# Zero-padded lower query tiles in the stick-breaking scores of a streaming encoder step

## The chip, the cores and the metric

The kernel runs on one NeuronCore of a Trainium2 chip. The metric is the device time of one execution in microseconds (us), the median of several runs. The engines are named as the profile names them: PE is TensorE's matrix multiply and PEld its load of the stationary operand, DVE is VectorE, ACT is ScalarE, POOL is GpSimd and SP is SyncE, which here only issues DMAs.

## The reference, cut to what matters

One layer of a hybrid encoder is computed for a prompt (1024 frames) and for 8 running streams (16 new frames each): an input projection, a spatial-gating branch, a stick-breaking attention with 8 heads of dimension 64, an output projection, a memory cross-attention and a SwiGLU. All is float32. What the change touches is the scores of the prompt's stick-breaking attention:

```python
z = jnp.einsum('bqhd,bkhd->bhqk', q, k) * (SB_HEAD_DIM ** -0.5)
mask = k_pos[None, :] < q_pos[:, None]
log_keep = jnp.where(mask, jax.nn.log_sigmoid(-z), 0.0)
between = lax.cumsum(log_keep, axis=3, reverse=True) - log_keep
a = jnp.where(mask, jnp.exp(jax.nn.log_sigmoid(z) + between), 0.0)
o = jnp.einsum('bhqk,bkhd->bqhd', a, v)
```

## The kernel before, in words

Float32 precision is reached with products of a rounded type (fp32r): each operand is split into an upper part, the rounded value, and a lower part, the rest, and two or three of the four products are summed in PSUM.

The queries of the prompt are written to a DRAM scratch `q_d[c, n, row, token]`: `c` counts pairs of heads, `n` is 0 for the upper and 1 for the lower part, and of the 128 rows the first 64 belong to the even head of the pair and the last 64 to the odd one. `k_d` has the keys in the same form. `head_in(h)` (lines 189 to 206) loads one head's operands with DMAs on SP's queue:

- `khl` (128 x 1024): the upper keys in the 64 rows that are the head's own (0 to 63 for an even head, 64 to 127 for an odd one), the lower keys in the other 64 rows.
- `qhh` (128 x 1024): the upper queries twice, in both halves.
- `ql` (128 x 1024): the lower queries of both heads of a pair, loaded once per pair by one DMA of 512 KB when the even head comes. Like `khl` and `qhh` it has two buffers.
- `vhl`: the values of both heads.

In `chunk` (line 423) the scores of 128 queries against a run of `w` keys (128 to 512) are two products in one PSUM bank (lines 430 and 431). The first, over 128 rows, has `qhh` as its stationary operand and `khl` as the moving one; it gives upper queries times upper and lower keys. The second contracts over the head's own 64 rows alone (`es`) and gives lower queries times upper keys. A head has 12 such chunks: 2 of 128 keys, 2 of 256, 2 of 384 and 6 of 512. With 8 heads that makes 96 pairs of products.

Behind them a chunk goes through a chain of engines (`sticks`, lines 391 to 408): DVE adds the causal mask, ACT takes two sigmoids, DVE scans the products (line 403), POOL multiplies (line 405), PE transposes the result (line 389, tile `tr`), ACT and DVE split it into `ath` and `atl` (line 126 and 127), and PE multiplies it by the values (`av`).

The order of the work is set by the loop at lines 726 to 742. Each turn starts one new chunk (or one stream of the 8) and takes every active one a step further; a chunk's transposes follow its scores by two turns (`LAG`). The rest of a turn is filled with products of other work (`memory` and then `merge_a`, tiles `acc`) until the turn has spent 4700 counted columns of PE time. The count takes the columns of a product, at least 256, and not its rows. `head_in(h + 1)` is called when head `h` begins (line 705, from head 1 on), that is when all score products of head `h - 1` have been issued, so that its loads wait for those to release a buffer and have the time of head `h` to land. The loads of heads 0 and 1 are issued earlier, beside the gating branch (lines 316 and 317). The framework that fills the engines' queues may place an instruction ahead of its place in the program where its inputs come earlier.

Of the kernel before, what the change touches and what calls it, by code (L numbers as in the profile page):

```python
# [9 lines left out]
F32 = mybir.dt.float32  # L10
F32R = mybir.dt.float32r
# [5 lines left out]
P = 128  # L17
# [4 lines left out]
NP = 1024  # L22
# [15 lines left out]
def stream_step(ctx: ExitStack, tc: tile.TileContext, I, O, cst):  # L38
    nc = tc.nc

    def pool(stack, name, bufs=1, **kw):
        return stack.enter_context(tc.tile_pool(name=name, bufs=bufs, reuse_waits="tile", **kw))
# [10 lines left out]
    def nm(s):  # L53
        uid[0] += 1
        return f"{s}_{uid[0]}"
# [5 lines left out]
    def ps(tag, shape):  # L61
        n = next(cur[tag])
        return psum[0].tile(shape, F32, tag=f"bank{n}", name=nm(tag))
# [17 lines left out]
    q_d = dram.tile([4, 2, P, TOK], F32, name="q_d")  # L81
# [39 lines left out]
    def split(hi, lo, src, gain=None):  # L121
        if gain is not None:
            nc.scalar.activation(hi, src, AF.Copy, scale=gain)
            nc.vector.scalar_tensor_tensor(out=lo, in0=src, scalar=gain, in1=hi.bitcast(F32), op0=ALU.mult, op1=ALU.subtract)
            return
        nc.scalar.copy(hi, src)  # L126
        nc.vector.tensor_tensor(out=lo, in0=src, in1=hi.bitcast(F32), op=ALU.subtract)  # L127
# [56 lines left out]

    stB = ctx.enter_context(ExitStack())
    bhp = pool(stB, "b_h", bufs=2, side="right")
    vhls, qls, got = [], [], {}

    def head_in(h):
        e, c2 = h % 2, h // 2  # L190
        if e == 0:
            ql = bhp.tile([P, NP], F32R, tag="ql", name=nm("ql"))
            nc.sync.dma_start(ql.bitcast(F32), q_d[c2, 1, :, 0:NP])
            qls.append(ql)
        es = slice(e * 64, e * 64 + 64)
        qhh = bhp.tile([P, NP], F32R, tag="qhh", name=nm("qhh"))
        khl = bhp.tile([P, NP], F32R, tag="khl", name=nm("khl"))
        for n in range(2):
            half = slice(n * 64, n * 64 + 64)
            nc.sync.dma_start(khl[half].bitcast(F32), k_d[c2, n ^ e, es, 0:NP])  # L200
            nc.sync.dma_start(qhh[half].bitcast(F32), q_d[c2, 0, es, 0:NP])
        if e == 0:
            vhl = bhp.tile([P, 8, 2, P], F32R, tag="vhl", name=nm("vhl"))
            nc.sync.dma_start(vhl.bitcast(F32), v_d[:, h:h + 2, :].rearrange("(n p) e d -> p n e d", p=P))
            vhls.append(vhl)
        got[h] = qhh, qls[-1], khl, vhls[-1]

    with ExitStack() as st:
        banks(acc=(1, 2), tr=(3, 4), z=(5, 6))
# [100 lines left out]
        for m in range(2):  # L310
# [3 lines left out]
            nc.vector.tensor_tensor(out=wsT[:, m], in0=tr, in1=trilT.unsqueeze(1).broadcast_to([P, 4, P]), op=ALU.mult)  # L314

        head_in(0)
        head_in(1)

        def sgu_v(i):
# [49 lines left out]
    with ExitStack() as st:  # L369
# [12 lines left out]
        def mm(out, lhsT, rhs, start, stop):  # L382
            n = math.prod(out.shape[1:])
            spent[0] += max(256, n) if rhs.dtype != F32 else 2 * max(256, 2 * n)
            nc.tensor.matmul(out, lhsT=lhsT, rhs=rhs, start=start, stop=stop)  # L385

        def tp_(out, in_, idn):
            spent[0] += 261
            nc.tensor.transpose(out, in_, idn)  # L389

        def sticks(w, zmm, right=None):
            beta = sp.tile([P, 512], F32, tag="beta", name=nm("beta"))
            pr = sp.tile([P, 513], F32, tag="pr", name=nm("pr"))
            z = ps("z", [P, 512])[:, :w]
            for _ in zmm(z):
                yield
            yield beta, pr
            nc.scalar.activation(z_keep(z, beta[:, :w]), z, AF.Sigmoid, scale=-0.125)
            if right is None:
                nc.gpsimd.memset(pr[:, w:w + 1], 1.0)  # L400
            else:
                nc.gpsimd.tensor_copy(pr[:, w:w + 1], right[:, 0:1])
            nc.vector.tensor_tensor_scan(out=pr[:, :w][:, ::-1], data0=z[:, ::-1], data1=zero1.broadcast_to([P, w]),  # L403
                                         initial=1.0 if right is None else right[:, 0:1], op0=ALU.mult, op1=ALU.add)
            nc.gpsimd.tensor_tensor(out=beta[:, :w], in0=beta[:, :w], in1=pr[:, 1:w + 1], op=ALU.mult)  # L405
            yield
            for _ in range(LAG - 1):
                yield
# [5 lines left out]
        def pair(h, c, got):  # L414

            sh = {}
            spans = [(512, 2 * c), (0, 2 * c)] if c >= 2 else [(0, 2 * c)]
            for part, (s, _) in enumerate(spans):
                for qb in (2 * c, 2 * c + 1):
                    e = (qb + 1) * P if part == 0 else 512  # L420
                    yield chunk(h, c, qb, s, e, part, len(spans) - 1, sh, got)

        def chunk(h, c, qb, s, e, part, last, sh, got):
            qhh, ql, khl, vhl = got[h]
            ev = h % 2
            es, col = slice(ev * 64, ev * 64 + 64), slice((qb % 2) * P, (qb % 2) * P + P)
            w, qs = e - s, slice(qb * P, (qb + 1) * P)

            def zmm(z):
                mm(z, lhsT=qhh[:, qs], rhs=khl[:, s:e], start=True, stop=False)  # L430
                mm(z, lhsT=ql[es, qs], rhs=khl[es, s:e], start=False, stop=True)
                if part == 0:
                    nc.vector.tensor_tensor(out=z[:, w - P:w], in0=z[:, w - P:w], in1=causal, op=ALU.add)
                return ()

            for step in sticks(w, zmm, sh.get(qb)):
                if step:
                    beta, sh[qb] = step
                yield
            if qb % 2 == 0:  # L440
                sh["ath"] = tp.tile([P, 4, 256], F32R, tag="ath", name=nm("ath"))
                sh["atl"] = tp.tile([P, 4, 256], F32R, tag="atl", name=nm("atl"))
            ath, atl = sh["ath"], sh["atl"]
            n = w // P
            tr = ps("tr", [P, 4, P])
            for j in range(n):
                tp_(tr[:, j, :], beta[:, j * P:(j + 1) * P], ident)
            split(ath[:, :n, col], atl[:, :n, col], tr[:, :n, :])
            yield
            if qb % 2 == 0:  # L450
                return
            if part == 0:
                sh["av"] = ps("av", [P, 256])
            av = sh["av"]
            for j in range(n):
                lo = P if part == 0 and j == n - 1 else 0
                for m, at in enumerate((ath, atl)):
                    mm(av[:, lo:], lhsT=vhl[:, s // P + j, ev, :], rhs=at[:, j, lo:],
                                     start=part == 0 and j == 0 and m == 0, stop=part == last and j == n - 1 and m == 1)
            yield  # L460
            if part == last:
                oe = sp.tile([P, 256], F32, tag="oe", bufs=1, name=nm("oe"))
                nc.scalar.copy(oe[0:64], av[64:128])
                nc.vector.tensor_tensor(out=oe[0:64], in0=av[0:64], in1=oe[0:64], op=ALU.add)
                nc.sync.dma_start(oT_d[h * 64:h * 64 + 64, c * 256:(c + 1) * 256], oe[0:64])
# [234 lines left out]
        def tasks():  # L700
            sgot[0] = stream_in(0)
            n, b = 0, 0
            for h in range(8):
                if 0 < h < 7:
                    head_in(h + 1)
                for c in range(4):
                    for g in pair(h, c, got):
                        yield g
                        n += 1
                        if n == S0 + SP * b and b <= B:  # L710
                            yield stream(b, sgot) if b < B else stream_tails(sgot[B])
                            b += 1
                        elif b and n == S0 + SP * (b - 1) + LAG + 6 and b <= B:
                            sgot[b] = stream_in(b)
# [637 lines left out]
```

## Time and profile before

| | |
|---|---|
| median of 3 runs | 1779.42 us (1777.08 to 1784.06) |
| the profiled execution | 1778.3 us, of which the span of the instructions is 1776.5 us |
| PE busy | 1718.3 us, 97% of the span |
| PEld busy | 1501.5 us, 85% |
| DVE busy | 987.3 us, 56% |
| ACT busy | 678.2 us, 38% |
| POOL busy | 435.4 us, 25% |
| the stick-breaking stage | 283 to 578 us of the span |

A busy PE isn't a PE at its peak: matmuls overlap their neighbours, so the duration of one is longer than the time to the next one's start. The time that an instruction takes from its engine is read from the starts of its followers. A weight load (PEld) can run beside the matmul ahead of it, and where one doesn't, its start coincides with that of its own matmul.

### The profile page before, as it was taken

What the parts mean: (1) busy time and instruction counts of PE and PEld (TensorE: products, weight loads), DVE (VectorE), ACT (ScalarE), POOL (GpSimd) and SP (SyncE); (2) the same over time, 40 slices, a digit from 0 to 9 for tenths busy, and PEclk for the clock granted to TensorE, in tenths of its full rate; (3) what the DMA queues carried; (4) which work ended last, traced back from release to release, by engine and by line L of the source; (5) the groups of instructions that cost most, each with busy time, mean ns of one, the idle gap of its engine ahead of it and who ended that gap; (6) DMA issues with size and microseconds to landing.
All of it is one profiled execution on the core that took longest, in us unless ns stands there. A gap on an engine that the chain in (4) does not pass through costs nothing.

```text
span 1776.5 us, 26280 instructions
## 1 busy us (share of the span) xinstructions
PE 1718.3 (97%) x10039; PEld 1501.5 (85%) x10039; DVE 987.3 (56%) x1481; ACT 678.2 (38%) x1326; POOL 435.4 (25%) x572
## 2 busy tenths in 40 slices
PE   8999999999999999998799799999999999999997
PEld 6889887776777799998687699999999999888886
DVE  5312446889778746455635855555555556544444
ACT  5322224767556436445522433333333333011123
POOL 2101233444333320000011444443444442000002
PEclk9999998999999999999899899999999999999999
DMA  8457236567543634344633122222222226322202
GB/s 287 148 187 257 68 125 193 154 195 231 184 117 113 209 107 131 116 127 141 210 119 119 48 75 75 75 75 75 75 75 75 75 80 239 141 101 101 101 13 95
DMA packets 175070, 227.94 MB, mean 128 GB/s; under 512 B 12065, under 2 KB 122273, under 8 KB 174945
## 3 DMA queue, kind: packets, MB, share of 16 engines
q1 hardware_dynamic: 143248, 161.89, 30.0%
q10 hardware_dynamic: 23504, 35.79, 5.5%
q0 software_dynamic: 8192, 28.58, 4.3%
q8 instruction: 80, 1.31, 0.3%
q14 instruction: 46, 0.37, 0.1%
HBM read 161.86 MB, written 64.36 MB: 127 GB/s over the span
## 4 chain that ended last, share of the span: by engine, by line
PE 65%; DVE 4%; DMA 2%; issue 2%; ACT 2%; POOL 1%; SPq 0%; POOLq 0%; ACTq 0%; DVEq 0%
PE pp L1158 27%; PE tr L131 5%; PE tr L130 5%; PE tr L132 5%; PE acc L385 3%; PE acc L130 2%; PE acc L131 2%; PE acc L132 2%; PE pp L130 2%; PE z L385 2%; PE pp L131 2%; PE pp L132 2%; PE tr L389 2%; PE av L385 1%; PE ov L943 1%
## 5 line engine op out<-in xcount | busy, mean ns | idle before, releaser
L1158 PE MATMUL pp<-b,wg 128*128 128x288 f32 x1584 | 223.3, 297 | 2.2 <-ACT b L126 1.9
L1158 PEld LDWEIGHTS pp<-b,wg 128*128 128x128 f32 x1584 | 215.2, 189 | 2.9 <-ACT b L126 2.3
L131 PE MATMUL tr<-wd,hid 128*128 128x512 f32 x396 | 154.6, 391 | 0.0
L132 PE MATMUL tr<-wd,hid 128*128 128x512 f32 x396 | 154.1, 389 | 0.0
L130 PE MATMUL tr<-wd,hid 128*128 128x512 f32 x396 | 151.5, 389 | 0.9 <-DVE t L1148 0.9
L127 DVE TENSOR_TENSOR wg<-s,wg 128x512 fp32r<-128x512 f32 x88 | 87.7, 996 | 103.4 <-ACT wg L126 102.5
L1293 DVE TENSOR_TENSOR xr<-tr,xr 128x512 f32<-128x512 f32 x108 | 73.3, 689 | 121.0 <-PE tr L132 117.6
L405 POOL TENSOR_TENSOR beta<-beta,pr 128x512 f32<-128x512 f32 (+4 forms) x104 | 95.6, 921 | 163.8 <-DVE pr L403 147.6
L130 PE MATMUL acc<-wh,hah 128*128 128x512 f32 x288 | 114.5, 398 | 2.6 <-ACT hah L126 2.6
L132 PE MATMUL acc<-wh,hal 128*128 128x512 f32 x288 | 113.7, 395 | 0.6 <-DVE hal L127 0.6
L131 PE MATMUL acc<-wl,hah 128*128 128x512 f32 x288 | 113.1, 393 | 0.0
L126 ACT CAST hid<-hr 128x576 fp32r<-128x576 f32 x44 | 27.3, 668 | 188.7 <-PE tr L132 177.8
L126 ACT CAST wg<-raw 128x512 fp32r<-128x512 f32 x66 | 41.0, 622 | 132.3 <-PE pp L1158 54.4
L130 PEld LDWEIGHTS tr<-wd,hid 128*128 128x128 f32 x396 | 74.4, 188 | 17.0 <-DVE t L1148 1.1
L131 PEld LDWEIGHTS tr<-wd,hid 128*128 128x128 f32 x396 | 74.3, 188 | 16.7 <-DVE wd L127 1.5
L132 PEld LDWEIGHTS tr<-wd,hid 128*128 128x128 f32 x396 | 74.4, 188 | 15.3
L126 ACT CAST wg<-s 128x512 fp32r<-128x512 f32 x88 | 54.2, 620 | 76.3 <-PE pp L1158 43.3
L1015 POOL DMA_DIRECT2D x_d<-xt x9 | 5.6, 627 | 312.8 <-DVE xt L1014 312.8
L1305 POOL TENSOR_SCALAR sm<-sm 128x1 f32<-128x1 f32 x9 | 7.1, 794 | 253.1 <-ACT junk L1298 253.1
L1078 POOL TENSOR_TENSOR s<-raw 128x512 f32<-128x512 f32 x22 | 28.9, 1315 | 156.0 <-DMA raw<-in_w_ffn_up_dram 75.4
L385 PE MATMUL acc<-mw,aT 128*128 128x512 f32 x216 | 66.8, 421 | 0.1
L127 DVE TENSOR_TENSOR wl<-raw,wh 128x1024 fp32r<-128x1024 f32 x36 | 43.7, 1221 | 41.0 <-ACT wh L126 40.4
(281 smaller groups left out, 4555.4 us busy)
## 6 DMA issues: line engine op xcount, KB each, us to landing
hid_d<-g ACTq DMA_DIRECT2D x44, 288.0 KB, 2.1
hr<-hid_d SPq DMA_DIRECT2D x44, 288.0 KB, 4.7
raw<-in_w_ffn_gate_dram SPq DMA_DIRECT2D x22, 512.0 KB, 3.9
raw<-in_w_ffn_up_dram SPq DMA_DIRECT2D x22, 512.0 KB, 4.0
raw<-in_w_ffn_down_dram SPq DMA_DIRECT2D x22, 512.0 KB, 4.5
raw<-in_w_in_dram SPq DMA_DIRECT2D x20, 512.0 KB, 5.1
x_d<-xt POOLq DMA_DIRECT2D x18, 512.0 KB, 3.1
raw<-in_cache_mem_k_dram SPq DMA_DIRECT2D x16, 512.0 KB, 4.4
```

Source lines behind the costliest of these rows:

```text
L126: nc.scalar.copy(hi, src)
L127: nc.vector.tensor_tensor(out=lo, in0=src, in1=hi.bitcast(F32), op=ALU.subtract)
L130: nc.tensor.matmul(out, lhsT=lh, rhs=rh, start=first, stop=False)
L131: nc.tensor.matmul(out, lhsT=lh, rhs=rl, start=False, stop=False)
L132: nc.tensor.matmul(out, lhsT=ll, rhs=rh, start=False, stop=last)
L385: nc.tensor.matmul(out, lhsT=lhsT, rhs=rhs, start=start, stop=stop)
L389: nc.tensor.transpose(out, in_, idn)
L405: nc.gpsimd.tensor_tensor(out=beta[:, :w], in0=beta[:, :w], in1=pr[:, 1:w + 1], op=ALU.mult)
L943: nc.tensor.matmul(ov[:, g], lhsT=pm[:, n, g, b4 * P:(b4 + 1) * P], rhs=vv[m][:, n], start=b4 == 0 and n == 0 and m == 0, stop=b4 == 3 and ...
L1078: nc.gpsimd.tensor_tensor(out=s[n], in0=x, in1=y, op=op)
L1158: nc.tensor.matmul(acc[:, h], lhsT=hl[:, a, c], rhs=b[:, c, h * TN:(h + 1) * TN], start=c == 0 and k == 0, stop=c == 3 and k == 2)
L1293: nc.vector.tensor_tensor(out=xr[i][:, hs], in0=pd, in1=xr[i][:, hs], op=ALU.add)
```

## The change

The lower queries stand in two fixed tiles, `qz0` for even heads and `qz1` for odd ones, each 128 x 1024 with one buffer. The half that isn't the head's own is set to zero once by POOL, when heads 0 and 1 are loaded. Each head loads its own 64 rows by a DMA of 256 KB, ahead of its `khl` and `qhh`. The second product of the scores then contracts over all 128 rows.

```diff
+    qzs = [bhp.tile([P, NP], F32R, name=f"qz{e}", bufs=1) for e in range(2)]
-    vhls, qls, got = [], [], {}
+    vhls, got = [], {}
 
     def head_in(h):
         e, c2 = h % 2, h // 2
-        if e == 0:
-            ql = bhp.tile([P, NP], F32R, tag="ql", name=nm("ql"))
-            nc.sync.dma_start(ql.bitcast(F32), q_d[c2, 1, :, 0:NP])
-            qls.append(ql)
         es = slice(e * 64, e * 64 + 64)
+        if h < 2:
+            nc.gpsimd.memset(qzs[e][64 - e * 64:128 - e * 64].bitcast(F32), 0.0)
+        nc.sync.dma_start(qzs[e][es].bitcast(F32), q_d[c2, 1, es, 0:NP])
...
-        got[h] = qhh, qls[-1], khl, vhls[-1]
+        got[h] = qhh, qzs[e], khl, vhls[-1]
...
-            es, col = slice(ev * 64, ev * 64 + 64), slice((qb % 2) * P, (qb % 2) * P + P)
+            col = slice((qb % 2) * P, (qb % 2) * P + P)
...
                 mm(z, lhsT=qhh[:, qs], rhs=khl[:, s:e], start=True, stop=False)
-                mm(z, lhsT=ql[es, qs], rhs=khl[es, s:e], start=False, stop=True)
+                mm(z, lhsT=ql[:, qs], rhs=khl[:, s:e], start=False, stop=True)
```

## Rows read from the trace of the kernel before

**Rows 1.** Windows, one per head: length, busy PE, PEld, DVE, ACT, POOL; clock, DMA.

```profile
283.00:325.43 42.43, 38.27 (x170) 26.99 (x168) 35.70 (x59) 28.10 (x61) 18.71 (x32) 0.88 0.68 216
325.43:363.32 37.89, 37.60 (x221) 28.24 (x219) 32.70 (x55) 26.37 (x62) 16.03 (x33) 1.00 0.54 152
363.32:399.44 36.12, 35.44 (x198) 25.90 (x196) 30.30 (x52) 24.42 (x56) 13.96 (x28) 1.00 0.71 215
399.44:429.48 30.04, 28.40 (x161) 19.24 (x159) 27.11 (x50) 23.39 (x55) 14.42 (x27) 1.00 0.69 217
429.48:465.78 36.30, 36.16 (x207) 26.59 (x205) 30.62 (x54) 21.39 (x52) 14.93 (x32) 1.00 0.76 231
465.78:501.35 35.57, 35.41 (x201) 26.07 (x199) 26.94 (x49) 19.55 (x48) 12.83 (x29) 1.00 0.46 141
501.35:539.04 37.69, 37.31 (x209) 26.80 (x208) 28.91 (x52) 19.42 (x49) 13.88 (x33) 1.00 0.42 120
539.04:578.30 39.26, 37.68 (x201) 28.39 (x201) 34.43 (x62) 24.34 (x52) 13.13 (x20) 1.00 0.34 110
```

**Rows 2.** Tile z: the lower products, duration in ns, first and last start, shapes.

```profile
L385 PE MATMUL z<-khl,ql x96: 322/491/792, 283.4 to 569.0; 64*128 64x512 f32 x48, 64*128 64x128 f32 x16, 64*128 64x256 f32 x16, 64*128 64x384 f32 x16
```

**Rows 3.** Timeline of PE, a pair of 512 keys: start us, duration us, instruction.

```profile
567.19 1.64 PE L385 MATMUL acc<-mw,aT 128*128 128x512 f32 x6
568.66 0.40 PE L385 MATMUL z<-khl,qhh 128*128 128x512 f32 x1
568.99 0.50 PE L385 MATMUL z<-khl,ql 64*128 64x512 f32 x1
569.42 0.55 PE L389 MATMUL tr<-csb,beta 128*128 128x128 f32 x3
```

**Rows 4.** Timeline of PEld, the weight loads of the same pair; in brackets idle before.

```profile
568.44 0.19 PEld L385 LDWEIGHTS z<-khl,qhh 128*128 128x128 f32 x1
568.99 0.18 PEld L385 LDWEIGHTS z<-khl,ql 64*128 64x128 f32 x1 [0.36 <-issue]
```

**Rows 5.** Timeline of PE, pairs of 128 and 256 keys, neighbours of those widths.

```profile
547.52 0.28 PE L385 MATMUL av<-ath,vhl 128*128 128x256 f32 x1
547.64 0.28 PE L385 MATMUL av<-atl,vhl 128*128 128x256 f32 x1
...
549.95 0.22 PE L385 MATMUL z<-khl,qhh 128*128 128x128 f32 x1
...
550.35 0.44 PE L389 MATMUL tr<-csb,beta 128*128 128x128 f32 x2
...
552.44 0.28 PE L385 MATMUL z<-khl,qhh 128*128 128x256 f32 x1
...
552.96 0.55 PE L389 MATMUL tr<-csb,beta 128*128 128x128 f32 x3
...
553.58 0.22 PE L385 MATMUL av<-ath,vhl 128*128 128x128 f32 x1
553.64 0.28 PE L385 MATMUL av<-atl,vhl 128*128 128x128 f32 x1
553.76 0.44 PE L385 MATMUL acc<-mw,aT 128*128 128x512 f32 x1
```

**Rows 6.** Waits of PEld, 283 to 578: waiter <- releaser, us, times, longest.

```profile
PEld z L385 <- issue: 28.1, 97, 0.7
```

**Rows 7.** Chain of waits behind the stage: start us, us, what.

```profile
578.30 5.57 DMA xt<-xa_d
```

**Rows 8.** Timeline of SP: upper-query loads of heads 2 and 7; start, issue time.

```profile
325.67 0.59 SPq L201 DMA_DIRECT2D qhh<-q_d  x1
...
501.67 0.59 SPq L201 DMA_DIRECT2D qhh<-q_d  x1
```

**Rows 9.** DMA issues of that form: size, median us to landing.

```profile
qhh<-q_d SPq DMA_DIRECT2D x16, 256.0 KB, 4.8
```

**Rows 10.** Groups of POOL, 282 to 300: a memset; busy us, mean ns.

```profile
L479 POOL MEMSET qbd<- 128x1024 f32 x1 | 1.0, 952 | 0.4 <-PE z L385 0.4
```

## The prediction

> **What bounds the kernel now.** I read the page's busy times first (PE 97% of the span), then the windows of the one stage that the change touches, cut where a head's first lower product starts [rows 1]. The reader is to see two things there. PE is busy for all but 0.1 to 0.7 us in five of the eight stretches, so what shortens PE's work there shortens the stretch. And DVE is second, busy for 76 to 90% of a stretch, so it has little room: in the two stretches where its share is 88 and 90% (the last and the fourth), PE already stands for 1.58 and 1.64 us, which is 4.0 and 5.5% of them.
>
> The second view is the timeline of one pair of products, from start to start. A run of six full products of 512 columns goes from 567.19 to 568.66, 0.245 us each [rows 3]. The pair of scores of the same width takes 0.33 us to the lower product's start and 0.43 us from there to the next instruction, 0.76 us for 0.49 us worth of columns. The third view says where the rest goes: the upper product's weights are loaded at 568.44, beside the product ahead of it (which ends its issue at 568.66), but the lower product's weights are loaded at 568.99, at the very start of their own product, after 0.36 us in which PEld waited for nothing the profile shows [rows 4]. This isn't one case: the same wait is booked 97 times for 28.1 us over the stage [rows 6], and there are 96 lower products [rows 2].
>
> **The change part by part.** *The lower product over 128 rows.* Its columns stay the same, its rows are all that changes, and every full-row product around it keeps pace with its columns. I take it that entering and leaving the 64-row form is what costs, and that a 128-row lower product is spaced like its neighbours. By width, start of the upper product to start of the next instruction, against two full-row products:
> - 512 keys: 0.76 - 2 x 0.245 = 0.27 us [rows 3], 48 pairs, 13.0 us.
> - 256 keys: 552.44 to 552.96 is 0.52; a full product of 256 takes 0.12 (547.52 to 547.64); 0.52 - 0.24 = 0.28 us, 16 pairs, 4.5 us [rows 5].
> - 128 keys: 549.95 to 550.35 is 0.40; two full products of 128 take 0.18 (553.58 to 553.76); 0.22 us, 16 pairs, 3.5 us [rows 5].
> - 384 keys: no row of a full product of this width; between its neighbours, 0.28 us, 16 pairs, 4.5 us.
>
> The sum is 25.5 us of PE time, 3.2 us per head. The bounds: nothing, if the gap belongs to something other than the rows (a rival below), and the 28.1 us of [rows 6], if no load of these products is left uncovered.
>
> *A rule that speaks against it.* Full-row loads do run beside a full-row product in this trace: the upper product's 0.19 us of loading at 568.44 lie before its own start at 568.66 [rows 3, 4]. The Trainium skill, "TensorE: Matmul & The Clock Gate", Part 3, "What overlaps and what doesn't", says that a weight load overlaps a matmul in flight only where their row groups differ; by that a 128-row load behind a 128-row product would stay uncovered, the pair would stay at about 0.76 us and the sum would be nothing. The rows contradict it for full-row neighbours.
>
> *What is late next.* 25.5 us less PE work raises DVE's share, as its work stays. Taking 3.2 us from every stretch of [rows 1], DVE would stand at 91, 94, 92, 101, 93, 83, 84 and 95% of them. From the two rows at 88 and 90% I take 5% of a stretch as PE's loss where DVE is over 90%, and count only what is added to the present loss: second stretch 1.7 - 0.3 = 1.4, third 1.6 - 0.7 = 0.9, fifth 1.7 - 0.1 = 1.6, last 1.8 - 1.6 = 0.2 us. The fourth can't be shorter than DVE's 27.11 us; with the same 5% it becomes 28.5 instead of 26.8, a loss of 1.7 us. The first loses 4.2 us now, mostly where the stage starts; I add 1.0 us. The sixth and seventh keep all. Together 6.8 us come back, and 25.5 - 6.8 = 18.7 us are left. From below this cost is nothing (DVE's stretches still have idle time in all but one), from above it takes nearly all in six stretches (rival below); I take the value nearest the two rows that show PE beside a DVE of this share.
>
> *The loads.* Eight DMAs of 256 KB replace four of 512 KB. Their nearest row is the upper queries' load, same size and rows: 0.59 us on SP's queue [rows 8] and 4.8 us to land [rows 9]. Four more issues are 2.4 us on SP over the program, spread over heads; behind them stand the head's other loads and the writes and stream loads of that turn, none of which is needed within a microsecond. The load waits for head h-1's last lower product, as the `khl` load beside it already does, so no new wait arises; it is only no longer a pair ahead. At head 2 a load issued near 325.67 has landed by some 332, and head 2 starts at 363.32; head 7's at 501.67 lands by some 507 for 539.04 [rows 1, 8, 9]. About 30 us cover it; cost nothing, and if that cover went, the wait would be PE's.
>
> *The two memsets.* The nearest row is a memset of 128 x 1024, 0.95 us on POOL [rows 10]; half the rows may take half as long or the same, so 1.0 to 1.9 us in all. They come ahead of loads whose data isn't read before 283 us, on an engine with 25% work; nothing on the path, 1.9 us if the cover is gone.
>
> *Behind the stage.* The chain goes on with the load of what the stage wrote last (578.30 [rows 7]), so all that follows moves with the stage's end, at the same length. I look for no change there. Neither the counted columns nor the turns change, so the order on PE should stay; small shifts in the order of SP and POOL could be worth a microsecond or two either way.
>
> **The sum.** The profiled execution took 1778.3 us (span 1776.5 and 1.8 around it); 1778.3 - 18.7 = 1759.6. It lies 1.1 us below the median of the runs, so for the median I say 1779.4 - 18.7 = 1760.7 us. About 0.5%, 9 us, is what a measurement of this kernel can tell from no change.
>
> **The rivals.**
> - *All of it arrives.* DVE's idle time in a stretch (3 to 9 us) absorbs the squeeze, since the chunks' transposes follow two turns behind. For it: at 84 to 86% DVE costs PE only 0.14 to 0.68 us in three stretches [rows 1]. Against: the fourth and the last. 25.5 to 28.1 us less: about 1752 us.
> - *DVE becomes the bound.* A chunk's scan and splits queue up on DVE, and PE waits for every turn's transposes. Then a DVE over 90% costs PE 10% of a stretch instead of 5%, which eats the 3.2 us of the first, second, fourth and fifth stretch and 2.6 and 2.0 us of the third and last, 17.4 us in all; 8.1 us are left: 1771 us. For it: the fourth and last stretch of [rows 1]. Against: no stretch loses over 6% now, apart from the first.
> - *The change doesn't do what it says.* The gap belongs to the second product of a bank or to its own weights, and the 128-row form keeps it: 1779 us. The rule of the skill above would have this. Against: runs of `acc` accumulate in one bank with new weights each at 0.245 us [rows 3].
> - *Slower.* The single buffer of `qz` is late: a head's lower queries load only when the head but one before has ended, and if they landed over 30 us after that, PE would wait at six heads. It decides for slower only where each wait is over 18.7 / 6 = 3.1 us; at 8 us each it is 6 x 8 - 18.7 = 29 us: 1809 us. For it: `ql` was loaded up to a pair ahead. Against: 30 us of cover [rows 1, 8, 9], on a release that `khl` shares.
>
> **How the numbers follow.** The forecast has 0.62, all of it 0.16, DVE as the bound 0.12, no effect 0.06, the late load 0.04. The forecast's own range is 1756 to 1766 (5% of a stretch taken as 3 to 7%). The range of 1751 to 1771 takes in the second case and the better half and more of the third, which leaves some 0.15 outside. Faster by over 0.5% means under 1770.5: the first two and two thirds of the third, 0.86. No change: the rest of the third and the fourth, 0.10. Slower 0.04.
>
> **What would show it.** Right: the 128-row lower weights are loaded before their product starts, the idle time of PEld ahead of `z` falls from 28 us to a few, and a pair of 512 takes 0.5 us to the next start; the stage ends 15 to 22 us earlier, DVE over 90% in most stretches, with new waits of PE's transposes and `av` on DVE and POOL. Wrong: pairs still at 0.76 us, a stage shorter by under 9 us, heads whose first lower product waits for a load, or a later stage whose length changes.

## The result, and the profile after

The changed kernel took 1769.97 us (median of 5 runs, 1768.94 to 1771.69) against 1778.34 for the kernel before: a ratio of 0.9948, 95% interval 0.9937 to 0.9960, 7 to 11 us. The profiled execution took 1768.94 us with a span of 1767.2, 9.3 us shorter than before. The forecast was 18.7 us.

The windows of the changed kernel, one per head, cut at the first score products of a head and closed where the first load of `xa_d` starts (578.30 before, 568.42 now), answer to [rows 1] (length, busy PE, PEld, DVE, ACT, POOL; clock, DMA):

```profile
285.80:328.68 42.88, 34.87 (x170) 27.37 (x169) 35.48 (x58) 28.55 (x62) 18.19 (x34) 0.88 0.67 213
328.68:365.04 36.36, 35.15 (x220) 28.68 (x220) 31.67 (x55) 25.87 (x61) 17.16 (x33) 1.00 0.57 169
365.04:399.91 34.87, 32.71 (x199) 25.58 (x197) 29.93 (x53) 23.46 (x55) 14.62 (x29) 1.00 0.75 214
399.91:430.62 30.71, 26.86 (x166) 20.22 (x166) 27.51 (x50) 23.80 (x56) 13.84 (x29) 1.00 0.74 223
430.62:464.84 34.22, 32.41 (x201) 26.14 (x199) 29.58 (x54) 21.19 (x50) 14.33 (x28) 1.00 0.72 226
464.84:497.90 33.06, 32.06 (x200) 26.09 (x199) 27.19 (x51) 19.75 (x48) 13.09 (x29) 1.00 0.58 168
497.90:531.84 33.94, 33.44 (x210) 27.00 (x209) 28.37 (x51) 19.42 (x49) 14.23 (x33) 1.00 0.46 140
531.84:568.42 36.58, 33.77 (x203) 28.70 (x202) 34.42 (x63) 24.38 (x52) 13.12 (x20) 1.00 0.38 118
```

PE's busy time in the stage fell from 286.3 us (the sum over [rows 1]) to 261.3, by 25.0. The stage itself fell from 295.3 to 282.6, by 12.7: PE stood still for 21.4 us of it instead of 9.0. The first four heads, 146.5 us before, took 144.8; the last four, 148.8 before, took 137.8. DVE's share is over 90% in one of the eight stretches, the last; the prediction looked for six.

The pair of products of 512 keys in the changed kernel's timelines of PE and, below it, of PEld, answering to [rows 3, 4]:

```profile
556.42 1.65 PE L385 MATMUL acc<-mw,aT 128*128 128x512 f32 x6
557.91 0.40 PE L385 MATMUL z<-khl,qhh 128*128 128x512 f32 x1
558.14 0.39 PE L385 MATMUL z<-khl,qz 128*128 128x512 f32 x1
558.37 0.49 PE L389 MATMUL tr<-csb,beta 128*128 128x128 f32 x3
```

```profile
557.67 0.19 PEld L385 LDWEIGHTS z<-khl,qhh 128*128 128x128 f32 x1
557.91 0.19 PEld L385 LDWEIGHTS z<-khl,qz 128*128 128x128 f32 x1
```

From the upper product's start to the next instruction it is 0.46 us where it was 0.76, and the lower weights are loaded at 557.91, while the upper product runs, 0.23 us ahead of their own. The waits of PEld in the stage, answering to [rows 6], say the same for all pairs:

```profile
PEld z L385 <- issue: 3.3, 13, 0.7
```

28.1 us in 97 waits have become 3.3 in 13. What PE then waits for shows in the waits of PE over the stage (waiter, releaser: us, times, longest). First the kernel before, then the changed one:

```profile
PE tr L389 <- DVE atl L127: 1.8, 3, 0.9
...
PE av L385 <- DVE atl L127: 0.7, 1, 0.7
...
PE z L385 <- DVE pr L403: 0.3, 1, 0.3
```

```profile
PE tr L389 <- DVE atl L127: 6.1, 8, 3.1
...
PE z L385 <- DVE pr L403: 2.8, 8, 0.9
PE av L385 <- DVE atl L127: 2.6, 3, 1.9
```

The transposes wait for DVE's split of an earlier chunk, the scores for DVE's scan of an earlier one, the value products for their own split.

A second change was not looked for: the program's start. DVE's timeline there, of the kernel before and of the changed one:

```profile
6.49 1.28 DVE L150 SCALAR_TENSOR_TENSOR xs<-xt,sm,gmix 128x1024 f32<-128x1024 f32 x1 [5.10 <-POOL sm L142]
```

```profile
9.45 1.23 DVE L127 TENSOR_TENSOR wl<-raw,wh 128x1024 fp32r<-128x1024 f32 x1 [8.05 <-ACT wh L126]
10.59 1.28 DVE L150 SCALAR_TENSOR_TENSOR xs<-xt,sm,gmix 128x1024 f32<-128x1024 f32 x1
```

In the changed kernel the first norm's scaling (`xs`) stands behind a weight split (`wl`) that waits for weights from HBM. POOL and PE at the same place, in the changed kernel:

```profile
0.92 1.94 POOL L194 MEMSET qz<- 64x1024 f32 x2
5.69 0.22 POOL L141 TENSOR_SCALAR sm<-sm 128x1 f32<-128x1 f32 x1 [2.82 <-ACT xs L148]
```

```profile
11.92 1.97 PE L159 MATMUL tr<-csb,xs 128*128 128x128 f32 x8 [3.83 <-DVE xs L150]
```

The two memsets end at 2.86 us and POOL is then idle for 2.8 us, so they delay nothing by their duration; yet the first transposes start at 11.92 us, and 7.83 before. (Around them the granted clock stands at 0.50, which is 1.2 GHz, from 10.8 to 17.6 us; in the kernel before from 13.1 to 16.5.) Of these 4.1 us 2.8 are left where the stage begins: the first lower product starts at 286.2 instead of 283.4 [rows 2].

Behind the stage the length changed by 0.6 us (windows from the stage's end to the last instruction, before and after):

```profile
578.30:1776.50 1198.20, 1155.46 (x7145) 1058.55 (x7143) 639.36 (x923) 403.20 (x750) 261.54 (x234) 0.99 0.33 106
```

```profile
568.42:1767.20 1198.78, 1155.28 (x7145) 1058.43 (x7143) 631.50 (x923) 401.02 (x750) 266.24 (x234) 0.99 0.33 106
```

So 2.8 - 12.7 + 0.6 = -9.3 us.

### The profile page after: what moved, and what is told of

Its sections match the earlier page's. It is cut to its first block, busy times and chain, and to the rows that moved or that the text cites. A ratio compares the mean times of both kernels' runs of the same rounds, so it can differ in the third digit from the quotient of the medians.

```text
span 1767.2 us, 26289 instructions
## 1 busy us (share of the span) xinstructions
PE 1694.3 (96%) x10039; PEld 1503.6 (85%) x10039; DVE 976.6 (55%) x1481; ACT 675.6 (38%) x1326; POOL 443.2 (25%) x574
## 4 chain that ended last, share of the span: by engine, by line
PE 58%; DVE 4%; DMA 3%; issue 2%; ACT 1%; POOL 1%; SPq 0%; POOLq 0%; ACTq 0%; DVEq 0%
PE pp L1158 27%; PE tr L131 5%; PE tr L130 5%; PE tr L132 5%; PE acc L131 2%; PE acc L132 2%; PE acc L130 2%; PE pp L130 2%; PE pp L131 2%; PE pp L132 2%; DMA or<-oT_d 2%; PE ov L943 1%; DMA raw<-in_cache_mem_v_dram 1%; PE ss L926 1%; PE tr L841 1%
## 5 line engine op out<-in xcount | busy, mean ns | idle before, releaser
L127 DVE TENSOR_TENSOR wg<-s,wg 128x512 fp32r<-128x512 f32 x88 | 79.0, 898 | 100.8 <-ACT wg L126 100.0
```

## The experiments

All times are medians with the ratio to the kernel before on the same chip; two runs on different chips are better compared by their ratios. The first three have the changed kernel's instruction order, the same on every engine, and differ from it only in the rows of some lower products. With the memsets on DVE PE's order in the stage is the changed kernel's too, and with the memsets alone it is that of the kernel before. In all other variants the framework laid the order on PE anew, so the edit isn't their only difference.

**64 rows again, all else changed.**

```diff
-                mm(z, lhsT=ql[:, qs], rhs=khl[:, s:e], start=False, stop=True)
+                mm(z, lhsT=ql[lr, qs], rhs=khl[lr, s:e], start=False, stop=True)
```

with `lr` the head's own 64 rows.

> The changed kernel with its zero tiles, loads and instruction order (the same on every engine), but each lower product contracts over the head's own 64 rows again. Theory (the products pay, the rest of the edit costs some 3 us at the program's start because the two memsets change the order of DVE there): 2 to 4 us slower than the kernel before, near 1781. Rival (the new order and loads in the stage are what costs 10 us or more, and the products give over 20): 1787 or slower. Rival (the gain comes from the order or the loads): 1772 or faster.

1783.31 us, ratio 1.0017 (1.0007 to 1.0028): 3.6 us slower than before. The 128-row products alone are worth 1783.31 - 1769.97 = 13.3 us by the medians and 12.3 by the ratios; the rest of the edit costs between 1 and 5. A part of this can be the clock: in the profiled execution the granted clock stood at 0.50 for 17.0 us of the stage (291.0 to 301.2 and 417.3 to 424.1), in that of the changed kernel for 10.2.

**128 rows in heads 0 to 3 alone, and in heads 4 to 7 alone.** `lr = slice(0, P) if h < 4 else slice(ev * 64, ev * 64 + 64)`, and `h >= 4`.

> As the changed kernel in order and loads, but 128-row lower products in heads 0 to 3 alone, 64 rows in heads 4 to 7. Theory (in the first four heads DVE's queue, which holds the splits of the memory weights, takes PE's saved time back): 0 to 3 us faster than the variant with 64 rows everywhere, about 1779. Rival (every head gives its share, half of the full effect): 5 to 6 us faster than that variant, about 1775.

> As the changed kernel in order and loads, but 128-row lower products in heads 4 to 7 alone. Theory: these four heads hold nearly all of the gain, 9 to 12 us faster than the variant with 64 rows everywhere, within 2 us of the changed kernel, about 1771. Rival (even shares): about 1775.

The first took 1776.76 us (0.9991, 0.9983 to 1.0000), 6.6 less than with 64 rows everywhere (4.6 by the ratios); the second 1774.25 us (0.9973, 0.9963 to 0.9984), 9.1 less (7.8). So the early heads give more than my theory had it and less than the late ones; both times lie nearer to the rival of even shares. The windows of heads 0 to 3 and 4 to 7, first with 64 rows everywhere, then with 128 in the late heads, then the changed kernel:

```profile
285.81:434.20 148.39, 142.76 (x738) 102.85 (x737) 124.19 (x212) 101.62 (x231) 62.78 (x119) 0.94 0.67 198
434.20:574.30 140.10, 138.87 (x765) 102.26 (x763) 112.00 (x205) 79.33 (x189) 49.95 (x106) 1.00 0.49 149
```

```profile
286.62:433.43 146.81, 140.43 (x738) 100.92 (x737) 124.07 (x212) 101.78 (x231) 63.05 (x119) 0.97 0.68 200
433.43:561.14 127.71, 124.84 (x765) 102.59 (x764) 110.02 (x204) 78.40 (x187) 49.91 (x105) 1.00 0.54 163
```

```profile
286.15:429.70 143.55, 128.32 (x739) 100.66 (x738) 123.67 (x212) 101.20 (x231) 63.53 (x119) 0.96 0.68 204
429.70:557.90 128.20, 124.88 (x764) 102.61 (x763) 109.97 (x204) 78.58 (x188) 50.08 (x106) 1.00 0.54 163
```

In the same order of instructions, PE's work falls by 14.4 us in the first half (part of that a difference in the clock, 0.94 and 0.96) and by 14.0 in the second. PE's idle time grows from 5.6 to 15.2 us in the first half and from 1.2 to 3.3 in the second. Up to the last upper product, where these windows end, the late heads keep 12 of 14 us, the early ones 4.8 of 14.4. Against the kernel before, whose clock in the first half was 0.96 as well, the early heads are 2.6 us shorter and the late ones 11.2. From the last upper product to the first result of the merge (line 785) it takes 15.6 us with 64 rows everywhere, 16.2 in the changed kernel and 19.0 with 128 rows in the late heads, where the clock stands at 0.50 from 566.4 to 573.2; so the late heads' gain isn't all kept either. (The profiled execution of the variant with 128 rows in the early heads took 1782.4 us, with the clock at half from 413.4 to 423.6; its windows can't be compared.)

**The memsets alone, in the kernel before.**

```diff
             ql = bhp.tile([P, NP], F32R, tag="ql", name=nm("ql"))
+            if h == 0:
+                for n in range(2):
+                    nc.gpsimd.memset(ql[64 - n * 64:128 - n * 64].bitcast(F32), 0.0)
```

> The kernel before with two memsets of 64 x 1024 on POOL into the first buffer of ql, ahead of its load, and nothing else changed. Theory (the memsets alone cost the first norm its place in DVE's order): the first transposes start 4 us later and the whole is 2 to 3 us slower than the kernel before. Rival (they are hidden, and the later start belongs to the new loads): no difference over 1 us.

1782.58 us, 1.0014 (1.0006 to 1.0023): 2.9 us slower. The first norm's scaling again stands behind the weight split, at 10.77 us, the first transposes start at 12.10, and the first lower product at 286.1 instead of 283.4. So the memsets alone bring this about, by the order of DVE and not by their duration. The variant with 64 rows everywhere, which has the new loads and the new order besides, is 0.7 us slower than this one by the medians; the intervals allow nothing as well as some 3 us.

**The memsets on DVE.** `nc.vector.memset` instead of `nc.gpsimd.memset` in the changed kernel.

> The changed kernel with the two memsets on DVE instead of POOL; the order of the first norm and weight splits on DVE is then that of the kernel before. Theory (2 to 3 us of the change's gain were lost at the start): first transposes near 8 us instead of 12, about 1767. Rival (the two memsets delay DVE by 2 us instead, or the later start is taken up elsewhere): 1770.

1766.85 us, 0.9932 (0.9918 to 0.9946). The interval overlaps that of the changed kernel, whose median is 3.1 us higher. The traces show more: the memsets take 0.91 us each on DVE at 1.66 and 2.83, the scaling starts at 6.54 and the first transposes at 7.88. In this profile the stage begins at 285.0, 1.7 us later than in the kernel before; 1.2 of them are lost by 22 us of the span, where the granted clock stands at 0.50 until 19.0 us instead of 16.5, and most of the rest between 140 and 146; why, isn't shown. Over all profiled executions the first upper product starts at 285.8 to 286.6 us in the six with the memsets on POOL, and at 282.7 to 285.0 in the eight without them or with them on DVE.

**Half of the memory weights' splits on POOL,** in that variant, and for comparison in the kernel before.

```diff
-            pend.append((hl[0][:, 1], hl[1][:, 1], raw[:, 1], gain))
+            pend.append((hl[0][:, 1], hl[1][:, 1], raw[:, 1], gain, nc.gpsimd))
```

> The variant with the memsets on DVE, and of the 20 memory weights of 1024 columns the second half's lower part is taken by POOL instead of DVE (line 127, some 20 instructions of 0.86 us off DVE, most of them in heads 0 to 3). Theory (in heads 0 to 3 PE waits for DVE's queue): the first four heads shorten by 3 to 8 us together, 1760 to 1764. Rival (what PE waits for there is weights from DMA, ACT, or the clock): within 1.5 us of the variant with the memsets on DVE.

> The kernel before with the same splits moved to POOL, nothing else. Theory (before the change PE set the pace and DVE had room): within 1.5 us of the kernel before, 1778 to 1780. Rival (DVE held the kernel before too): 3 us or more faster.

1765.18 us, 0.9919 (0.9906 to 0.9932): at most a little faster than with the memsets on DVE. The kernel before took 1783.32 us with it, 1.0017 (1.0007 to 1.0027), slower, which neither expectation had; in its profiled execution the clock falls (below). Heads 0 to 3 with the splits on DVE and half on POOL:

```profile
284.98:426.62 141.64, 128.21 (x738) 100.75 (x737) 123.26 (x212) 101.27 (x231) 63.54 (x119) 0.96 0.69 207
```

```profile
284.08:424.15 140.07, 127.04 (x738) 101.04 (x737) 110.75 (x192) 101.45 (x231) 84.44 (x136) 0.95 0.69 210
```

DVE is freed of 12.5 us, and PE's idle time goes from 13.4 to 13.0. PE's waits for DVE do fall, but new ones take their place. The waits of PE in heads 0 to 3, half on POOL:

```profile
PE acc L385 <- POOL mw L127: 2.6, 1, 2.6
...
PE tr L389 <- DVE atl L127: 1.0, 3, 0.4
```

The transposes' waits for `atl` were 5.5 us with the splits on DVE. The theory expected heads 0 to 3 to shorten by 3 to 8 us, and they shorten by 1.6. That doesn't clear DVE's load, though: POOL took over the same splits, and some 21 us into the stage, near the place of the longest wait for `atl` (3.1 us), PE now waits 2.6 us for one of POOL's.

**The lower products left out,** the count of columns kept.

```diff
-                mm(z, lhsT=qhh[:, qs], rhs=khl[:, s:e], start=True, stop=False)
-                mm(z, lhsT=ql[:, qs], rhs=khl[:, s:e], start=False, stop=True)
+                mm(z, lhsT=qhh[:, qs], rhs=khl[:, s:e], start=True, stop=True)
+                spent[0] += max(256, w)
```

> The changed kernel without the lower products: scores from the upper queries alone, 96 products less, the turn's count of columns kept. That takes some 18 us more PE work out of the stage. Theory (PE's work now beyond what DVE can follow in heads 0 to 3): of the 18 us 6 to 11 are gained, most of it in heads 4 to 7, about 1761. Rival (PE still sets the pace everywhere): 16 us or more, 1754 or less.

1752.40 us, 0.9846 (0.9834 to 0.9859), 17.6 us less than the changed kernel. The time is the rival's, but its reason isn't shown: PE doesn't set the pace everywhere, as heads 0 to 3 show, and the order is another one, so it isn't the products alone. The windows of heads 0 to 3:

```profile
286.20:419.40 133.20, 122.24 (x697) 94.53 (x696) 123.43 (x213) 100.38 (x230) 66.03 (x119) 0.95 0.70 212
```

DVE does the same work at 93% of the stretch, and PE stands still for 11.0 us; in the changed kernel DVE's share is 86% and PE stands still for 15.2. Over the whole stretch a DVE of 86% isn't at its bound.

**Turns of 5000 and of 4300 counted columns** instead of 4700, with the memsets on DVE.

> The variant with the memsets on DVE and turns of 5000 counted columns instead of 4700, so that other products fill each turn a little longer. Theory (PE's waits in heads 0 to 3 are a matter of place in the queues, not of DVE's total work: a shorter pair brings the transposes up sooner than DVE and POOL have done their part, and a longer turn gives the time back): PE's waits in heads 0 to 3 fall from 13 us to 10 or less, the filling runs out sooner and the last heads lose some of it; 1763 to 1767. Rival (DVE's total work sets the pace there): heads 0 to 3 stay within 1 us of 141.6.

> As before with turns of 4300 counted columns. Theory (place in the queues): the transposes come up sooner still, PE's waits in heads 0 to 3 grow by 3 us or more, 1768 to 1775. Rival (DVE's total work): the heads' lengths move with the filling that is shifted out of them, and PE's waits in sum stay within 2 us.

1771.24 us (0.9952, 0.9938 to 0.9966) and 1773.65 us (0.9968, 0.9958 to 0.9979). Heads 0 to 3 took 147.9 and 130.9 us, as more or less other work fills them. With the longer turn PE's idle time there stays at 13.4 us; with the shorter one it falls:

```profile
283.86:414.78 130.92, 119.97 (x714) 94.34 (x712) 119.10 (x204) 94.78 (x220) 62.11 (x115) 0.97 0.67 191
```

10.9 us, with DVE at 91%. Both are against the theory that a longer turn gives the chain its time back, and the second also against DVE's total work as the bound. The whole is slower than with turns of 4700 in the second; in the first it is 4.4 us slower by the medians, and the intervals overlap a little.

**The first five weights' splits on DVE, half of the others on POOL.** `nc.gpsimd if j > 4 else None` in the diff above.

> The variant with half the splits on POOL, but the first five weights' splits stay on DVE, so that POOL's queue is free for the first chunks. Theory (place in the queues): the wait of 2.6 us for POOL near 305 goes, and of the waits of PE for DVE in head 0 the longest (3.1 us) is back; 1763 to 1766. Rival (the relief of DVE is worth nothing in itself): 1767 as with all on DVE.

1766.79 us, 0.9927 (0.9915 to 0.9940), no different from either neighbour. The wait for POOL went, and the longest wait of the transposes for `atl` came back at 4.2 us, as expected; PE's idle time in heads 0 to 3 is 14.7 us, and the time tells nothing apart.

**Three banks for the transposes, two for the scores,** with the memsets on DVE.

```diff
-        banks(acc=(1, 2), z=(5, 6, 7), tr=(3, 4), av=(0,), first=(0, 7))
+        banks(acc=(1, 2), z=(5, 6), tr=(3, 4, 7), av=(0,), first=(0, 7))
```

> The variant with the memsets on DVE, in which the chunks' transposes have three PSUM banks instead of two and the scores two instead of three. Theory (what PE waits for in heads 0 to 3 is a bank: the transposes may not start before DVE's split has emptied the bank of the chunk two before): the waits of PE's transposes for atl fall from 5.5 us to 2 or less there, those of the scores for DVE's scan grow from 2.3 us by more than that, since the scan frees a bank later; 1767 to 1775. Rival (the transposes wait for their own data or for DVE in general): the waits for atl stay at 5 us or more, the time at 1767.

1771.79 us, 0.9961 (0.9947 to 0.9974); the profiled execution, with 1764.7 us, is the fastest of the six. The waits of PE in heads 0 to 3, with the banks as before and then exchanged:

```profile
PE tr L389 <- DVE atl L127: 5.5, 6, 3.1
...
PE z L385 <- DVE pr L403: 2.3, 7, 0.9
```

```profile
PE z L385 <- DVE pr L403: 5.1, 9, 1.8
...
PE av L385 <- DVE atl L127: 2.5, 2, 2.3
```

With a third bank no wait of the transposes for `atl` is left; the scores, a bank short, wait 2.8 us more for the scan that empties theirs, and 2.5 us now show as value products that wait for their own `atl`. So the transposes did wait for a bank, but the bank isn't what keeps PE: the value product behind the transposes needs the same split of DVE, and at the place where the transposes had waited 3.1 us it now waits 2.25 us (timeline of PE):

```profile
304.28 0.49 PE L389 MATMUL tr<-csb,beta 128*128 128x128 f32 x3
...
307.38 0.39 PE L385 MATMUL av<-atl,vhl 128*128 128x256 f32 x1 [2.25 <-DVE atl L127]
```

PE's idle time in heads 0 to 3 is 15.2 us, not less than the 13.4 with two banks. That the scores' waits grew by more than the transposes' shrank, as expected, didn't come out.

## Why the prediction was right or wrong

The 1770.0 us lie inside the prediction's wide range (1751 to 1771) by 1 us and outside the forecast's own (1756 to 1766); the gain is half of the 18.7 us forecast. That the wide range held is luck as far as the forecast goes: it reached so far for the sake of a rival.

**The pairs: right.** 25.5 us less PE work were forecast; the stage's windows give 25.0. A pair of 512 lost 0.30 us where 0.27 was forecast. Over all pairs at full clock and without a wait the medians went from 0.75 to 0.47 us (512 keys), 0.64 to 0.35 (384), 0.52 to 0.24 (256) and 0.41 to 0.17 (128), which makes 26.5 us for the 96. The weight load of the 128-row lower product does run beside a full-row product in flight (557.91), so the rule of the Trainium skill that the prediction weighed doesn't hold for these rows. The trace shows a gap ahead of the 64-row product and a longer one behind it. The Trainium skill, "TensorEngine Tiling (Array Packing)", section "Key Properties", says that changing the tiling mode drains TensorE; if a 64-row product among 128-row ones counts as such a change, each lower product was two of them. The gaps fit that, about 0.3 us for the two; a drain itself no run here shows, and the page gives no price.

**What is late next: wrong in size, and in how it was priced.** 6.8 us were to come back; 12.3 did (PE idle for 21.36 instead of 9.02 us), 8.5 of them in heads 0 to 3 (9.6 against the variant with 64 rows everywhere, which has the same order). I had priced it by DVE's share of a stretch. The runs show that this share sets no such price: 93 and 91% of DVE go with 11.0 and 10.9 us of PE's idle time in heads 0 to 3, 86 and 87% with 15.2 and 13.4, and taking 12.5 us off DVE changed 13.4 to 13.0. PE waits for single instructions that stand late in DVE's queue. The largest wait in the changed kernel, on DVE and then on PE:

```profile
305.26 3.94 DVE L127 TENSOR_TENSOR mw<-raw,mw 128x512 fp32r<-128x512 f32 x4
309.13 0.41 DVE L127 TENSOR_TENSOR atl<-tr,ath 128x256 fp32r<-128x256 f32 x1
```

```profile
306.16 0.40 PE L385 MATMUL acc<-mw,mTh 128*128 128x512 f32 x1
309.68 0.52 PE L389 MATMUL tr<-csb,beta 128*128 128x128 f32 x3 [3.13 <-DVE atl L127]
309.96 0.36 PE L385 MATMUL av<-atl,vhl 128*128 128x256 f32 x1
```

Four weight splits in a row stand ahead of the split that empties the transposes' bank and that the next value product needs. The windows over the same DVE instructions, in the kernel before and in the changed one:

```profile
299.07:306.05 6.98, 6.98 (x30) 5.33 (x29) 6.98 (x11) 3.70 (x7) 5.43 (x6) 0.94 0.79 249
```

```profile
302.49:309.46 6.97, 4.07 (x20) 3.06 (x18) 6.97 (x10) 3.70 (x7) 5.42 (x6) 1.00 0.72 226
```

For these 7 us DVE has no gap in either kernel, though its share of the whole first stretch is 84 and 83%: PE kept up with it before and stands still for 2.9 us now. With 64-row products the same order cost PE 0.5 us at this place (at 309.28), as its own work lasted longer; a part of that is the clock, which stood at half until 301.2 us there and until 297.5 in the changed kernel. What stays open is why such places gather in heads 0 to 3, and what an order laid for the faster pair would give back: neither turns of another length, nor splits moved to POOL, nor other banks brought PE's idle time there under 10.9 us, and the run without lower products, which had another order, kept the whole of what it saved.

The prediction also expected the order on PE to stay. In the traces it doesn't, from some 349 us of the span on. That isn't what PE's new waits come from: with 64 rows everywhere and the new order PE stands still for 5.6 us in heads 0 to 3, and for 6.8 in the kernel before.

**The memsets: wrong.** They were priced at nothing, 1.9 us if their cover went. Their 1.94 us are hidden, but they moved the first norm behind a weight split in DVE's order, and the stage began 2.8 us later. The prediction allowed a microsecond or two for shifts in the order of SP and POOL and didn't look at DVE.

**The loads: right.** No wait of PE names a load of `qz`, and the loads and the new order together cost 0.7 us over the memsets by the medians, which isn't clear of nothing. **Behind the stage: right** within 0.6 us, 1198.2 before and 1198.8 after.

**The rivals.** The late single buffer and the pair that keeps its gap are excluded by the rows above. The time came out where the rival with DVE as the bound had put it (1771), but by another way: DVE isn't over 90% in most stretches, and PE doesn't wait for every turn's transposes (8 waits of theirs for `atl` in the stage). Of the 9.4 us that are missing, 5.5 are idle time of PE beyond the 6.8 forecast, 2.8 the program's start, 0.6 the part behind the stage and 0.5 PE work that I had counted too many.

## What to carry to other kernels

Two products that alternate between full and half rows pay for each change of form: look for weight loads that start together with their own product, multiply the gap by their count, and a half of zeros can be cheaper than the half left out (here 0.46 instead of 0.76 us for a pair of 512 keys). Before booking the gain in full, follow, instruction by instruction, the engine whose results the faster engine will ask for sooner; its share of busy time over a long stretch doesn't tell, as it can be full for 7 us within it. An instruction that costs nothing by its duration can still change the order that a planner lays out on another engine; here that happened at the start of the program, where nothing covered it.

## What was not expected of the hardware

The granted clock of TensorE fell in a stretch in which PE was busy. The windows around 416 us of the kernel before with half the splits on POOL, then of the kernel before:

```profile
405.00:415.90 10.90, 10.53 (x60) 7.63 (x58) 7.47 (x17) 7.86 (x20) 5.89 (x11) 1.00 0.79 259
415.90:429.55 13.65, 12.96 (x43) 9.41 (x44) 10.60 (x16) 9.11 (x20) 4.53 (x8) 0.50 0.55 169
```

```profile
405.00:415.90 10.90, 10.86 (x63) 8.09 (x62) 10.03 (x20) 7.60 (x19) 5.11 (x11) 1.00 0.75 255
415.90:429.55 13.65, 12.07 (x68) 7.65 (x66) 12.46 (x21) 11.91 (x26) 6.58 (x11) 1.00 0.66 206
```

Ahead of the fall PE was busy for 10.53 of 10.90 us and had issued 60 products; then it ran at half clock (1.2 GHz) for 13.65 us, 43 products instead of 68. In the kernel before, with 10.86 us and 63 products ahead, it stayed at 2.4 GHz. In the execution with the fall PE was busy for 145.0 us in heads 0 to 3 instead of 139.3; that the other executions of this variant are slower for the same reason isn't shown. Such falls come in other traces too, at other lengths (417.3 to 424.1 with 64 rows everywhere, 413.4 to 423.6 with 128 rows in the early heads), so a difference of a few microseconds between two profiled executions can be the clock's. Which property of the stretch decides isn't shown by these runs.
